# The first loads of an encoder step: x in contiguous blocks of 512 KB, with the first weights whole between them

## The chip, the cores and the metric

The kernel runs on one core of a Trainium2 chip. A core has a matrix engine (TensorE, PE in the profile, its weight loads PEld), three engines for elementwise work (VectorE or DVE, ScalarE or ACT, GpSimd or POOL), SyncE (SP), which here only issues transfers, and 16 DMA engines between the chip's memory and the core's own. The metric is the device time of one execution in microseconds; lower is better. The time before is the median of three runs.

## The reference

The reference is one inference step of a small streaming encoder of two layers, for 512 frames of a new stream and 8 x 16 frames of running streams: 640 tokens of 1024 channels in all.

```
layer 0: x = LN(a*x + 0.5*swiglu(x));  x = LN(a*x + [S5 | stick-breaking attention](x));  x = LN(a*x + 0.5*swiglu(x))
layer 1: x = LN(a*x + 0.5*swiglu(x));  x = LN(a*x + SSD(x));                              x = LN(a*x + 0.5*swiglu(x))
swiglu(x) = (silu(x @ w_gate) * (x @ w_up)) @ w_down        # w_gate, w_up: 1024 x 2816, w_down: 2816 x 1024
```

It returns the tokens and the states of the mixers. The change concerns the start of the first swiglu alone: the first products `x @ w_gate` and `x @ w_up`.

## The kernel before

**Tiles.** All matmuls are made in float32 precision out of three products of a narrower format: every operand `a` is split into `hi`, a rounded copy that ScalarE makes, and `lo = a - hi`, a subtraction on VectorE (`split`, L100). `mm3` (L146) then adds hi x hi, lo x hi and hi x lo in one accumulator bank. x lies in the core by channel: `xt["hi"]` and `xt["lo"]` hold 8 blocks of 128 channels (index `k`) by 640 tokens, and they are worked on in two token halves, tokens 0 to 255 and 256 to 639 (`HALVES`, L28). A weight unit is 128 output rows by 1024 input channels, 512 KB, and is loaded by `load_w` (L117) into one of four raw tiles (`RAWS`), then split in two halves of 512 columns each: half `j` serves channel blocks 4j to 4j + 3.

**Order.** The code is written out by hand. Each engine takes its instructions in program order, and a framework inserts the waits for data and for free buffers. Transfers are issued by SyncE in program order; one that waits for a free raw tile holds up those behind it. So where `load_x` and `load_w` stand in the program sets the order of the transfers, of the casts on ScalarE and of the subtractions on VectorE.

**The start.** `ffn` (L251) begins, for the first phase, with the lines L290 to L304. For the first token half, x comes by `load_x(0, ...)` (L1891) in four pieces of two channel blocks, 256 KB, each staged in a tile of the pool `h` (four buffers of 128 x 1280, which the hidden rows `ht` use later). The order of the transfers is: x blocks 0 and 1; the first half of the first w_gate unit; x blocks 2 to 5 in two pieces; the second half of that unit; x blocks 6 and 7; then whole units: w_up 0, w_gate 1, w_up 1. The casts follow in the order x 0-1, x 2-3, x 4-5, weights half 0, weights half 1, x 6-7, because `load_w` splits its halves only after both transfers and what lies between them. Then `load_rest` (L1899) loads the second token half of x in four pieces of 384 KB into raw tiles, and x by token into `yacc`.

In the memory of the chip, x by channel (`xT`, built by `_layout`) is an array of 128 rows; a row holds, for one position within its block, all 8 blocks of the first token half and then all 8 of the second: 20 KB. A piece of 256 KB is 128 runs of 2 KB, one out of each row.

The matmuls of the first projection (`by_k`) go channel block by channel block, with its three products each, so that they can begin when block 0 and half 0 of the weights are split; those of all others go product by product. Before them stand seven matmuls of the identity matrix with itself (L1914), whose result is used nowhere; the first real matmul is ordered behind them.

Of the kernel before, what the change touches and what calls it, by code (L numbers as in the profile page):

```python
# [25 lines left out]
KT = 8  # L26
NF = 22
HALVES = ((0, 256), (256, 384))  # L28
# [10 lines left out]
def kernel(ctx: ExitStack, tc: tile.TileContext, I, O, phases=PHASES):  # L39
    nc = tc.nc  # L40
# [31 lines left out]
    def bank_a():  # L72
        return bank(next(state["a"]))

    def bank_b():
        return bank(next(state["b"]))
# [7 lines left out]
    state = {"silu": None, "preload": None, "pst": bank_b}  # L84
# [15 lines left out]
    def split(hi, lo, src):  # L100
        nc.scalar.copy(hi, src)  # L101
        return nc.vector.tensor_tensor(lo, src, hi.bitcast(F32), op=ALU.subtract)  # L102

    def raw_tile():
        return pools["raw"].tile([128, 1024], F32, name="raw")
# [4 lines left out]
    def two_units():  # L110
        return pools["w"].tile([128, 2, 2, 512], F32R, name="w")
# [2 lines left out]

        return split(w[:, :, 0], w[:, :, 1], src.rearrange("p (j c) -> p j c", j=2))

    def load_w(src, rows=None, between=None):  # L117

        r = raw_tile()
        if between is None:  # L120
            nc.sync.dma_start(r, src)
        else:
            nc.sync.dma_start(r[:, :512], src[:, :512])
            between()
            nc.sync.dma_start(r[:, 512:], src[:, 512:])
        w = two_units()
        for j in range(2):
            half = r[:, 512 * j:512 * j + 512]
            if rows is None:
                split(w[:, j, 0], w[:, j, 1], half)  # L130
            else:
                nc.scalar.mul(w[:, j, 0], half, rows)
                nc.vector.scalar_tensor_tensor(w[:, j, 1], half, rows, w[:, j, 0].bitcast(F32),
                                               op0=ALU.mult, op1=ALU.subtract)
        return w[:, 0], w[:, 1]
# [22 lines left out]
    xt = {n: act.tile([128, KT, T], F32R, name="x" + n) for n in ("hi", "lo")}  # L158
# [92 lines left out]
    def ffn(i, ph, last, side=None):  # L251
# [4 lines left out]
        with ExitStack() as st:  # L256
# [34 lines left out]
            stage = lambda: wk.tile([128, 2 * T], F32, name="h", bufs=4)  # L291
            wg = {}
            if late:
                load_x(0, (0,), stage)
            for f in fs:
                between = (lambda: load_x(0, (2, 4), stage)) if late and f == 0 else None
                wg[f] = [load_w(I["w_gate"][i, f], None, between)]
                if between:
                    load_x(0, (6,), stage)
                wg[f].append(load_w(I["w_up"][i, f]))  # L300
            for f in fs:
                ht[f] = h_tile()
# [2 lines left out]
            for h in range(2):  # L305
                o, L = HALVES[h]
# [15 lines left out]
            for r in range(2):  # L322
                with tc.issue_after(state["xc"]) if "xc" in state else ExitStack():
                    w = load_w(I["w_gate"][i, 2 + r])
                first[r] = g_row()
                for c in range(2):
                    p = bank_a()[:, :Q] if r else sums[c]
                    mm3(p, [w_k(w, k) for k in range(KT)],
                        [(xh[:, k, Q * c:Q * c + Q], xl[:, k, Q * c:Q * c + Q]) for k in range(KT)])
                    state["silu"] = nc.scalar.activation(first[r][:, Q * c:Q * c + Q], p, AF.Silu).ins  # L330
# [1557 lines left out]
                    run_pend()  # L1888


    def load_x(h, ks=range(0, KT, 2), stage=raw_tile):  # L1891
        o, L = HALVES[h]
        for k in ks:
            r = stage()[:, :2 * L].rearrange("p (k c) -> p k c", c=L)
            state["load"] = nc.sync.dma_start(r.rearrange("p k c -> p (k c)"),
                                              I["xT"][:, KT * o + k * L:KT * o + (k + 2) * L]).ins
            split(xt["hi"][:, k:k + 2, o:o + L], xt["lo"][:, k:k + 2, o:o + L], r)

    def load_rest():  # L1899
        load_x(1)  # L1900
# [4 lines left out]
    late = [load_rest]  # L1905
# [5 lines left out]
    share("azay", "b")  # L1911

    pw = bank_b()
    for _ in range(7):  # L1914
        state["first"] = nc.tensor.matmul(pw[:, 0:128], ident, ident, start=True, stop=True).ins
    if "mix0" in phases and "ffn0" not in phases:
        with ExitStack() as st:
# [7 lines left out]
    for ph in phases:  # L1925
        last = ph == phases[-1]
        if ph.startswith("ffn"):
            ffn(int(ph[3]), ph, last, sides.get(ph))
        elif ph == "mix0":
            mixer0(ph, last)  # L1930
        else:
            mixer1(ph, last)
            if "ffn3" not in phases:
                with ExitStack() as st:
                    for _ in ssd_states(pool("ssd", 1, st, reuse_waits="tile")):
                        pass
# [4 lines left out]
def _layout(inp):  # L1941
    import numpy as np

    c = np.ascontiguousarray
    a = {k: np.asarray(v) for k, v in inp.items()}
    x = np.concatenate([a["x_prompt"].reshape(TP, D), a["x_sample"].reshape(T - TP, D)], 0)

    def cm(w):

        K, N = w.shape  # L1950
        return c(w.reshape(K // 128, 128, N // 128, 128).transpose(2, 1, 0, 3).reshape(N // 128, 128, K))

    def chan(v, n):
        return c(v.reshape(n, 128).T)

    def pairs(v):

        r = v.shape[2:]
        v = v.reshape((16, 2, 64) + r)
        return c(np.moveaxis(v, 0, 2).reshape((128, 16) + r))  # L1960

    xT = x.T.reshape(KT, 128, T).transpose(1, 0, 2)
    o = {"x": c(x), "xT": c(np.concatenate([xT[:, :, o:o + n].reshape(128, KT * n) for o, n in HALVES], 1))}
    o["ln_gb"] = c(np.stack([a["ln_g"].reshape(6, D), a["ln_b"].reshape(6, D)], 1))
    wg = a["ffn_w_gate"].reshape(4, D, NF * 128)
    wu = a["ffn_w_up"].reshape(4, D, NF * 128)
    o["w_gate"] = c(np.stack([cm(w) for w in wg]))
    o["w_up"] = c(np.stack([cm(w) for w in wu]))
    o["w_down"] = c(a["ffn_w_down"].reshape(4, NF, 128, D))

    w = cm(a["mix0_w_in"][0])
    order = [0, 1, 2, 3] + [4 + 4 * n + p for p in range(4) for n in range(2)]
    o["m0_in"] = c(w[order])
    o["m0_v"] = c(a["mix0_w_in"][0][:, 1536:].reshape(4, 2, 128, 512).transpose(0, 2, 1, 3).reshape(4, 128, 1024))
    o["m0_out"] = c(a["mix0_w_out"][0].reshape(8, 128, D))
    g = cm(a["s5_w_glu"][0])
    o["s5_wglu"] = c(g.reshape(2, 2, 128, 512).transpose(0, 2, 1, 3).reshape(2, 128, 1024))
    o["s5_bglu"] = chan(a["s5_b_glu"][0], 4)
    ldt = np.broadcast_to(a["s5_log_dt"][0][:, None], (32, 64))
    o["s5_par"] = c(np.stack([pairs(a["s5_a_re"][0]), pairs(a["s5_a_im"][0]), pairs(ldt)], 1))  # L1980
    cre = a["s5_c_re"][0].transpose(0, 2, 1)
    cim = a["s5_c_im"][0].transpose(0, 2, 1)
    o["s5_bc"] = c(np.stack([pairs(a["s5_b_re"][0]), pairs(a["s5_b_im"][0]), pairs(cre), pairs(cim)], 1))
    o["s5_d"] = c(a["s5_d"][0].reshape(1, 512))
    o["s5_h0"] = c(np.stack([pairs(a["state_s5_re"][0].transpose(1, 2, 0)), pairs(a["state_s5_im"][0].transpose(1, 2, 0))], 1))
    kc = a["cache_sb_k"][0][:, ::-1].reshape(8, 256, 4, 128)
    o["kcT"] = c(kc.transpose(2, 3, 0, 1))
    vc = a["cache_sb_v"][0][:, ::-1].reshape(8, 2, 128, 4, 128)
    o["vc"] = c(vc.transpose(3, 2, 0, 1, 4))

    w = a["ssd_w_in"][0]
    z, xbc, wdt = cm(w[:, :2048]), cm(w[:, 2048:5120]), w[:, 5120:]
    units = []
    for g in range(4):
        units += [xbc[16 + g], xbc[20 + g]] + [xbc[4 * g + q] for q in range(4)] + [z[4 * g + q] for q in range(4)]
    o["m1_in"] = c(np.stack(units))
    o["m1_dt"] = c(wdt.reshape(8, 128, 32).transpose(1, 0, 2).reshape(128, 256))
    o["m1_out"] = c(a["ssd_w_out"][0].reshape(16, 128, D))
    cwb = np.concatenate([a["ssd_conv_w"][0], a["ssd_conv_b"][0][None]], 0)
    o["conv_wb"] = c(cwb.reshape(5, 24, 128).transpose(2, 1, 0))  # L2000
    o["conv_st"] = c(a["state_conv"][0].reshape(8, 3, 24, 128).transpose(3, 2, 0, 1).reshape(128, 24, 24))
    dsk = np.repeat(a["ssd_d"][0], 64)
    o["ssd_ch"] = c(np.stack([chan(dsk, 16), chan(a["ssd_norm_g"][0], 16)], 1))
    o["ssd_hd"] = c(np.stack([a["ssd_dt_bias"][0], a["ssd_a_log"][0]], 1))
    o["ssd_h0"] = c(a["state_ssd"][0].reshape(8, 4, 512, 128).transpose(1, 0, 3, 2))
    return o
# [43 lines left out]
```

## Time and profile before

| | us |
|---|---|
| median of 3 runs (lowest, highest) | 2527.58 (2524.32, 2527.81) |
| the profiled execution, its own time | 2523.28 |
| its span, first to last instruction | 2521.6 |
| TensorE busy | 2483.8 |
| VectorE busy | 2011.8 |
| ScalarE busy | 1272.6 |
| first idle matmul of the identity starts | 1.59 |
| first matmul of the projection starts | 8.43 |
| mean granted TensorE clock | 0.998 |

The profile is one execution. Times within it count from the start of the span. In a row of the timeline stand the start, the length, the engine, the line, the operation, the written tile and the read ones with their shapes, a count, and in brackets the idle time of the engine before it with what ended it. Most lines of the first microseconds are those of helpers: L101 is the cast and L102 the subtraction of `split`, L153 the matmul of `mm3`.

### The profile page before, as it was taken

What the parts mean: (1) busy time and instruction counts of PE and PEld (TensorE: products, weight loads), DVE (VectorE), ACT (ScalarE), POOL (GpSimd) and SP (SyncE); (2) the same over time, 40 slices, a digit from 0 to 9 for tenths busy, and PEclk for the clock granted to TensorE, in tenths of its full rate; (3) what the DMA queues carried; (4) which work ended last, traced back from release to release, by engine and by line L of the source; (5) the groups of instructions that cost most, each with busy time, mean ns of one, the idle gap of its engine ahead of it and who ended that gap; (6) DMA issues with size and microseconds to landing.
All of it is one profiled execution on the core that took longest, in us unless ns stands there. A gap on an engine that the chain in (4) does not pass through costs nothing. (4 is left out here: it accounts for less than half of the span.)

```text
span 2521.6 us, 40821 instructions
## 1 busy us (share of the span) xinstructions
PE 2483.8 (99%) x15555; PEld 2281.2 (90%) x15555; DVE 2011.8 (80%) x3507; ACT 1272.6 (50%) x2390; POOL 378.7 (15%) x493
## 2 busy tenths in 40 slices
PE   9999999999999999999999999999999999999998
PEld 8999999878789999999999999999989879999997
DVE  7788777676879888877988887777586789998887
ACT  4444344336744555553455554566565544554542
POOL 0000001210130000013000001311121152211121
PEclk9999999999999999999999999999999999999999
DMA  5332334443222433452144434456464723455563
GB/s 187 109 101 79 115 116 158 145 151 118 86 77 67 115 106 98 113 157 74 59 113 113 115 105 134 150 164 199 150 215 135 244 74 100 155 148 168 154 171 115
DMA packets 178517, 324.80 MB, mean 129 GB/s; under 512 B 21344, under 2 KB 90976, under 8 KB 177808
## 3 DMA queue, kind: packets, MB, share of 16 engines
q1 hardware_dynamic: 164464, 293.83, 36.5%
q0 software_dynamic: 13856, 28.35, 5.8%
q8 instruction: 122, 2.00, 0.3%
q14 instruction: 75, 0.61, 0.1%
HBM read 259.56 MB, written 40.54 MB: 119 GB/s over the span
## 5 line engine op out<-in xcount | busy, mean ns | idle before, releaser
L101 ACT CAST w<-raw 128x512 fp32r<-128x512 f32 (+1 forms) x721 | 533.7, 771 | 332.4 <-DVE raw L376 143.4
L102 DVE TENSOR_TENSOR w<-raw,w 128x512 fp32r<-128x512 f32 (+2 forms) x721 | 621.2, 883 | 85.7 <-ACT w L101 82.8
L393 PE MATMUL bank<-xhi,w 128*128 128x320 f32 x2432 | 436.0, 309 | 2.2 <-DVE s L435 1.4
L393 PE MATMUL bank<-T,w 128*128 128x320 f32 x2736 | 428.3, 309 | 3.5 <-ACT bank L410 1.5
L393 PEld LDWEIGHTS bank<-T,w 128*128 128x128 f32 x2736 | 406.8, 188 | 6.7 <-ACT bank L410 4.2
L393 PEld LDWEIGHTS bank<-xhi,w 128*128 128x128 f32 x2432 | 376.7, 188 | 6.4 <-DVE s L435 2.2
L153 PE MATMUL bank<-xhi,w 128*128 128x256 f32 (+2 forms) x2272 | 362.8, 310 | 6.3 <-ACT w L101 3.5
L153 PEld LDWEIGHTS bank<-xhi,w 128*128 128x128 f32 x2272 | 335.9, 188 | 15.9 <-issue 4.6
L153 PE MATMUL bank<-w,h 128*128 128x512 f32 (+1 forms) x1500 | 346.5, 389 | 0.2 <-DVE yacc L239 0.2
L153 PEld LDWEIGHTS bank<-w,h 128*128 128x128 f32 x1500 | 277.8, 188 | 57.5 <-ACT h L101 1.6
L393 PE MATMUL bank<-xlo,w 128*128 128x320 f32 x1216 | 227.7, 309 | 0.0
L376 DVE TENSOR_TENSOR raw<-raw 128x512 f32<-128x512 f32 x304 | 214.2, 704 | 3.4
L393 PEld LDWEIGHTS bank<-xlo,w 128*128 128x128 f32 x1216 | 190.8, 188 | 0.0
L153 PE MATMUL bank<-xlo,w 128*128 128x256 f32 (+2 forms) x1136 | 190.4, 308 | 0.0
L542 POOL DMA_DIRECT2D yacc<-ev x84 | 72.8, 898 | 690.8 <-ACT ev L541 624.4
L153 PEld LDWEIGHTS bank<-xlo,w 128*128 128x128 f32 x1136 | 171.6, 187 | 0.6
L529 PE MATMUL bank<-w,h 128*128 128x512 f32 x576 | 134.5, 389 | 0.0
L529 PEld LDWEIGHTS bank<-w,h 128*128 128x128 f32 x576 | 107.8, 188 | 22.8 <-DVE yacc L538 0.6
L406 ACT COPY mx<-bank 128x320 f32<-128x320 f32 x152 | 64.7, 426 | 105.8 <-PE bank L393 104.9
L239 DVE SCALAR_TENSOR_TENSOR yacc<-bank,yacc 128x512 f32<-128x512 f32 x118 | 80.5, 687 | 39.7 <-PE bank L153 39.0
L538 DVE SCALAR_TENSOR_TENSOR yacc<-bank,yacc 128x512 f32<-128x512 f32 x84 | 57.9, 689 | 67.4 <-PE bank L529 67.4
L153 PE MATMUL bank<-w,og 128*128 128x512 f32 x432 | 104.6, 398 | 0.0
(442 smaller groups left out, 3360.0 us busy)
## 6 DMA issues: line engine op xcount, KB each, us to landing
raw<-in_w_up_dram SPq DMA_DIRECT2D x88, 512.0 KB, 3.9
raw<-in_w_down_dram SPq DMA_DIRECT2D x88, 512.0 KB, 3.6
raw<-in_w_gate_dram SPq DMA_DIRECT2D x87, 512.0 KB, 3.6
raw<-in_m_in_dram SPq DMA_DIRECT2D x52, 512.0 KB, 4.5
yacc<-ev POOLq DMA_DIRECT2D x84, 256.0 KB, 4.7
raw<-in_m_out_dram SPq DMA_DIRECT2D x24, 512.0 KB, 4.8
csb<-cs_d SPq DMA_DIRECT2D x20, 512.0 KB, 5.0
h<-in_ssd_h_dram SPq DMA_DIRECT2D x16, 512.0 KB, 6.4
```

The source lines that it names most:

```text
L101: nc.scalar.copy(hi, src)
L102: return nc.vector.tensor_tensor(lo, src, hi.bitcast(F32), op=ALU.subtract)
L153: state["pe"] = nc.tensor.matmul(ps, a, b, start=(k == 0), stop=(k == n - 1)).ins
L239: state["acc"] = nc.vector.scalar_tensor_tensor(ya, pb, scale, ya, op0=ALU.mult, op1=ALU.add).ins
L376: V.tensor_tensor(o, v, w, op=ALU.subtract)
L393: nc.tensor.matmul(ps, A[p][:, a, k * 128:k * 128 + 128], X[p][b][:, k, :], start=(first and n == 0), stop=(n == 11), skip_group_check=True)
L406: nc.scalar.copy(e[n], ps)
L529: nc.tensor.matmul(ps, a[:, u], b[:, v], start=(first and n == 0), stop=(n == 5), skip_group_check=True)
L538: V.scalar_tensor_tensor(ya, ps, 0.5 / ALPHA, ya, op0=ALU.mult, op1=ALU.add)
L542: nc.gpsimd.dma_start(yacc[:, t, 512 * j:512 * j + 512], e, accum_op=ALU.add)
```

## The change

x by channel is stored so that each transfer is one contiguous block: two blocks of 4 channel blocks (512 KB) for the first token half, four blocks of 2 channel blocks (384 KB) for the second. The first token half is loaded in these two transfers, each into one staging tile, and split by two casts and two subtractions of the old shape. The first w_gate unit is loaded whole, between the two. So the transfers are x 0-3, w_gate 0, x 4-7, w_up 0, w_gate 1, w_up 1; the casts go x 0-1, x 2-3, weights half 0, weights half 1, x 4-5, x 6-7. `load_w` loses the argument that let other loads stand between its two halves. Nine matmuls of the identity stand at the start instead of seven.

```diff
-    def load_w(src, rows=None, between=None):
+    def load_w(src, rows=None):
 
         r = raw_tile()
-        if between is None:
-            nc.sync.dma_start(r, src)
-        else:
-            nc.sync.dma_start(r[:, :512], src[:, :512])
-            between()
-            nc.sync.dma_start(r[:, 512:], src[:, 512:])
+        nc.sync.dma_start(r, src)
...
             if late:
-                load_x(0, (0,), stage)
+                load_x(0, (0,), 4, stage)
             for f in fs:
-                between = (lambda: load_x(0, (2, 4), stage)) if late and f == 0 else None
-                wg[f] = [load_w(I["w_gate"][i, f], None, between)]
-                if between:
-                    load_x(0, (6,), stage)
+                wg[f] = [load_w(I["w_gate"][i, f])]
+                if late and f == 0:
+                    load_x(0, (4,), 4, stage)
                 wg[f].append(load_w(I["w_up"][i, f]))
...
-    def load_x(h, ks=range(0, KT, 2), stage=raw_tile):
+    def load_x(h, ks=range(0, KT, 2), n=2, stage=raw_tile):
         o, L = HALVES[h]
         for k in ks:
-            r = stage()[:, :2 * L].rearrange("p (k c) -> p k c", c=L)
-            state["load"] = nc.sync.dma_start(r.rearrange("p k c -> p (k c)"),
-                                              I["xT"][:, KT * o + k * L:KT * o + (k + 2) * L]).ins
-            split(xt["hi"][:, k:k + 2, o:o + L], xt["lo"][:, k:k + 2, o:o + L], r)
+            r = stage()[:, :n * L]
+            src = I["xT"][128 * (KT * o + k * L):128 * (KT * o + (k + n) * L)]
+            state["load"] = nc.sync.dma_start(r, src.rearrange("(p c) -> p c", p=128)).ins
+            r = r.rearrange("p (k c) -> p k c", c=L)
+            for m in range(0, n, 2):
+                c = slice(k + m, k + m + 2)
+                split(xt["hi"][:, c, o:o + L], xt["lo"][:, c, o:o + L], r[:, m:m + 2])
...
-    for _ in range(7):
+    for _ in range(9):
         state["first"] = nc.tensor.matmul(pw[:, 0:128], ident, ident, start=True, stop=True).ins
...
-    o = {"x": c(x), "xT": c(np.concatenate([xT[:, :, o:o + n].reshape(128, KT * n) for o, n in HALVES], 1))}
+    o = {"x": c(x), "xT": c(np.concatenate([xT[:, k:k + n, o:o + L].reshape(-1)
+                                                  for (o, L), n in zip(HALVES, (4, 2)) for k in range(0, KT, n)]))}
```

## The prediction

> **What bounds the kernel now.** I read the page first, then the waits of TensorE, then the first 25 us engine by engine, and last the granted clock in single windows.
>
> ```profile
> span 2521.6 us, 40821 instructions
> ...
> PE 2483.8 (99%) x15555; PEld 2281.2 (90%) x15555; DVE 2011.8 (80%) x3507; ACT 1272.6 (50%) x2390; POOL 378.7 (15%) x493
> ```
>
> TensorE is busy for 99% of the span: 2521.6 - 2483.8 = 38 us are idle. The change only touches code that runs in the first microseconds, so it can only work on the idle time there and on the pace there. The waits of TensorE in the first 30 us, and its busy time once its stream has begun (columns of the second view: stretch, its length, PE busy, instructions, granted clock, DMA share, GB/s):
>
> ```profile
> PE bank L153 <- ACT w L101: 3.5, 1, 3.5
> PE bank L153 <- DVE w L102: 0.2, 1, 0.2
> ```
>
> ```profile
> 9.23:60.00 50.77, 50.77 (x321) 1.00 0.53 187
> 60.00:200.00 140.00, 139.87 (x854) 1.00 0.32 102
> ```
>
> From 9.23 us to 60 us TensorE never stops, and to 200 us it loses 0.13 us. So what the first projection gains passes on to what follows, as long as no later operand comes out late. The timeline of TensorE (start, length, line):
>
> ```profile
> 1.59 3.36 PE L1915 MATMUL bank<-ident 128*128 128x128 f32 x14 [1.59 <-POOL ident masks.py:199]
> 8.43 0.58 PE L153 MATMUL bank<-xhi,w 128*128 128x256 f32 x1 [3.48 <-ACT w L101]
> 9.23 0.58 PE L153 MATMUL bank<-xhi,w 128*128 128x256 f32 x1 [0.22 <-DVE w L102]
> ...
> 11.75 0.63 PE L153 MATMUL bank<-xhi,w 128*128 128x256 f32 x2
> ...
> 12.81 0.28 PE L153 MATMUL bank<-xlo,w 128*128 128x256 f32 x1
> ...
> 13.61 1.98 PE L153 MATMUL bank<-xhi,w 128*128 128x256 f32 x16
> ...
> 21.77 0.51 PE L153 MATMUL bank<-xhi,w 128*128 128x384 f32 x2
> ```
>
> Seven idle matmuls (14 instructions, 0.24 us each) end at 4.95; the first real one starts at 8.43 and the continuous stream at 9.23. One more thing is to be read here: two matmuls of 256 columns take 0.63 us at 11.75, with steps of 0.21 us from one to the next ((12.81 - 11.75)/5), and sixteen later take 1.98, 0.12 each. TensorE runs at half pace until about 12.8. What holds the first matmul is seen on ScalarE and VectorE:
>
> ```profile
> 3.98 0.62 ACT L101 CAST xhi<-h 128x512 fp32r<-128x512 f32 x1 [1.89 <-DMA h<-in_xT_dram]
> 5.96 0.62 ACT L101 CAST xhi<-h 128x512 fp32r<-128x512 f32 x1 [1.36 <-DMA h<-in_xT_dram]
> 7.24 0.62 ACT L101 CAST xhi<-h 128x512 fp32r<-128x512 f32 x1 [0.66 <-DMA h<-in_xT_dram]
> 7.76 1.34 ACT L101 CAST w<-raw 128x512 fp32r<-128x512 f32 x2
> 9.11 0.62 ACT L101 CAST xhi<-h 128x512 fp32r<-128x512 f32 x1
> 10.40 3.67 ACT L101 CAST w<-raw 128x512 fp32r<-128x512 f32 x6 [0.67 <-DMA raw<-in_w_up_dram]
> ...
> 18.18 1.56 ACT L101 CAST xhi<-raw 128x768 fp32r<-128x768 f32 x2
> ```
>
> ```profile
> 8.49 1.33 DVE L102 TENSOR_TENSOR w<-raw,w 128x512 fp32r<-128x512 f32 x2
> 9.76 0.69 DVE L102 TENSOR_TENSOR xlo<-h,xhi 128x512 fp32r<-128x512 f32 x1
> ```
>
> The weights' cast stands behind three casts of x in ScalarE's order, and the third x piece arrives only at 7.24. From the start of the weights' cast it is 8.43 - 7.76 = 0.67 us to the first matmul and 9.23 - 7.76 = 1.47 us to the stream (the subtraction on VectorE in between).
>
> **The change, part by part.** The loads first: SyncE's issues, and the time from issue to landing of single transfers (last column, us).
>
> ```profile
> 0.81 0.39 SPq L1895 DMA_DIRECT2D h<-in_xT_dram  x1
> 1.25 0.42 SPq L123 DMA_DIRECT2D raw<-in_w_gate_dram  x1
> ...
> 3.61 0.43 SPq L121 DMA_DIRECT2D raw<-in_w_up_dram  x1
> ```
>
> ```profile
> h<-in_xT_dram SPq DMA_DIRECT2D x1, 256.0 KB, 3.2
> ...
> raw<-in_w_gate_dram SPq DMA_DIRECT2D x1, 256.0 KB, 3.3
> ...
> raw<-in_w_up_dram SPq DMA_DIRECT2D x1, 512.0 KB, 6.8
> ```
>
> So 256 KB had landed at 0.81 + 3.2 = 4.0, 512 KB at 1.25 + 3.3 = 4.55, 1024 KB at 7.24 (the third x cast's wait), 1536 KB by 9.1, 2048 KB at 3.61 + 6.8 = 10.4. What the DMA engines moved between:
>
> ```profile
> 3.50:5.00 1.50, 1.45 (x7) 1.00 0.86 212
> ...
> 8.00:11.00 3.00, 2.35 (x9) 1.00 1.02 414
> ```
>
> At nearly equal busy share the early stretch moves half as much. There pieces of x lie in the queue, each 2 KB per partition out of a row of 20 KB; later whole weight units of 4 KB per partition.
>
> Issues: six transfers ahead of the first w_up unit become three, about 0.45 us of SyncE each, so w_up's issue moves from 3.61 to about 0.81 + 3 x 0.46 = 2.2; what stands behind on that queue is issued 1.4 us earlier. Worth nothing by itself, since the DMA engines have work throughout.
>
> First x block, 512 KB instead of 256 KB: it lands as late as the first 512 KB did, 4.55. The two casts of x can then start 0.57 us later than the first did, at 4.55 and, casts of this shape following each other by 7.76 - 7.24 = 0.52, at 5.07; ScalarE is free at 5.6. This costs nothing while the weights land after 5.6.
>
> First weights whole, second in the queue, so at 1024 KB in all. Upper end: 7.24 as before. Lower end: 512 KB at the late rate, 524/414 = 1.27 us after 4.55, that is 5.82. How a compact block of x fares the trace does not show; compact weights reach 414 GB/s, but not at the start of the program. I take the middle, 6.4 (an estimate). The stream then starts at 6.4 + 1.47 = 7.87 instead of 9.23: **1.36 us earlier**, between 0.52 (7.24, only the third x cast taken out from ahead of the weights) and 1.94.
>
> One rule speaks on this term: the Trainium skill, page "DMA: Bandwidth & Descriptors" (Specifications), puts the ceiling of all 16 engines at 435 GB/s; the late row is close to it, the early one at half. At that ceiling for the whole of the first megabyte the weights would land before ScalarE is free, and the stream would start at about 5.6 + 1.47 = 7.07 (an estimate).
>
> x channels 4 to 7 after the weights: 1536 KB, at worst 9.1 as before; cast to 9.7 and subtracted to 10.5. At half pace channels 0 to 3 take TensorE from 7.87 to 7.87 + 11 x 0.21 = 10.2. So at worst the stream waits 0.3 us, and by the middle (about 8, 6.4 plus the mean of 1.27 and the 9.1 - 7.24 = 1.9 of before) not at all: 0. The next unit, w_up, is cast from 10.4 at the latest and its subtraction is needed after the 24 + 8 matmuls of gate: no wait.
>
> Second token half: four blocks of 384 KB, same bytes per partition, same slots. They wait for a raw tile, which VectorE frees after the weights' subtraction, and come about as much earlier as that. The casts of x end at 19.7, the matmuls that read them begin at 21.77: 2 us of cover, and both move together. 0.
>
> Two staging tiles of the pool instead of four: the two tiles of the first hidden rows take fresh buffers instead of reused ones; nothing waits there today. 0.
>
> Two more idle matmuls: 4 x 0.24 = 0.96 us, ending at 5.91, ahead of the first real one at 7.07 (5.82 + 0.67 = 6.49 at the lower end). They delay nothing; what they do to the pace is the last term. The granted clock, in windows of 3.41 us (PE busy in the third column, clock in the fifth; in the first windows the column holds 1.00, but the pace above says half):
>
> ```profile
> 2.55:5.96 3.41, 2.40 (x12) 1.00 0.91 281
> ```
>
> ```profile
> 664.73:668.14 3.41, 0.64 (x12) 1.00 0.49 165
> 668.14:671.55 3.41, 3.41 (x14) 0.50 0.00 0
> ...
> 2026.65:2030.06 3.41, 1.66 (x21) 1.00 0.11 31
> 2030.06:2033.47 3.41, 3.41 (x9) 0.50 0.45 123
> ```
>
> ```profile
> 1753.41:1756.83 3.42, 2.01 (x12) 1.00 0.83 283
> 2081.06:2084.48 3.42, 2.03 (x18) 1.00 0.04 7
> 575.93:579.34 3.41, 2.07 (x16) 1.00 0.00 0
> 2156.15:2159.56 3.41, 2.15 (x15) 1.00 0.23 28
> ```
>
> Windows with 0.64 and 1.66 us of work were followed by exactly one window at half clock; those with 2.01 or more were not. Counting back from 668.14 in steps of 3.413, 192 of them end at 12.8, where the pace doubles: so the same grid rules the start, and the window 2.55 to 5.96 with 2.40 busy did not open the clock. On this grid the changed kernel has the idle matmuls in that window from 2.55 to 5.91, 3.36 of 3.41, which I take as enough: full pace from 5.96. The next window, to 9.37, holds 0.11 + 9.37 - 7.87 = 1.61 us of work, just under the 1.66 that closed it: half pace from 9.37 to 12.78. Work done by 12.78, in full-pace time: 1.50 + 3.41/2 = 3.21, against (12.78 - 9.23)/2 = 1.78 before. **Gain 1.43 us**. If the idle matmuls do not open the clock: (12.78 - 7.87)/2 = 2.46, gain 0.68. The grid will lie otherwise in another execution; I take 1.4 as the sum.
>
> **The sum.** The profiled execution took 2523.28 us, its span 2521.6; less 1.4 gives 2521.9. The runs shown have a median of 2527.58, 4.3 above that execution, and all four together a mean of 2525.75. Less 1.4 these give 2526.2 and 2524.35; I take the point between, **2525.2**.
>
> **The rivals.**
>
> *The clock stays open.* If TensorE's work of 1.61 us between 5.96 and 9.37 is enough, or the weights land by 6.0 (then it is over 2.0, which the rows show to be enough), full pace holds from the first real matmul: 12.78 - 7.87 - 1.78 = 3.1 us gained, with weights at 6.0 3.5. Time: 2525.75 - 3.3 = 2522.5 to 2527.58 - 3.3 = 2524.3. For it: the margin is 0.05 us. Against: the weights' landing must be in the faster half. The Trainium skill, page "TensorE: Matmul & The Clock Gate" (Part 1), has the clock fall back only after a whole idle window; by that the gate would stay open here and the gain would be 3.1. The row of 2026.65 disagrees: 1.66 us of work, and half clock after it.
>
> *Nothing lands earlier.* If the early 212 GB/s come from the start of the program and not from the pieces, the weights land at 7.24, the stream starts at 8.71, and on a grid that does not favour it the gain is (9.23 - 8.71)/2 = 0.3: 2527.3. For it: the first x piece, alone in the queue, took 3.2 us too. Against: six transfers become three.
>
> *Slower, by the clock later on.* The four windows of 2.01 to 2.15 us busy are near the closing point. If the shift of all work against the grid puts each a few tenths lower (the point lies between 1.66 and 2.01), each costs 3.41/2 = 1.7 us: four cost 6.8, less 1.4 is 5.4 slower, 2533.0. For it: two windows closed already. Against: the idle gaps there are as long as before, and a shifted grid can as well free the two that close now, 3.4 us.
>
> **How the numbers follow.** The forecast has 0.60, the open clock 0.20, nothing earlier 0.14, slower 0.06. What this kernel's measurement can tell from no change is 0.2%, 5 us. Below 2522.5 lie a tenth of the forecast's cases (the runs shown differ by 3.5 us among themselves) and a quarter of the open clock's: faster 0.11. Above 2532.6 half of the slow case and a little else: slower 0.04. The same 0.85. Range: from the open clock on a low run, 2520.5, to nothing gained on a high one, 2529.
>
> **What would show it.** The timeline of ScalarE: casts x, x, weights, weights, x, x, the third starting at about 6.4 (5.8 to 7.3). TensorE: 18 idle instructions to 5.9, the stream from 7.9 (7.3 to 8.7) without a wait of over 0.3 us; the pace in the first channels, 0.64 or 0.34 us per channel, tells the clock. The start of the second token half's matmuls, at 21.77 before, shows the whole gain of this stretch: 20.4 by the forecast, 18.5 with the clock open. Wrong I am if TensorE waits anew between 9 and 200 us, if x's second block comes after 9.1, or if that start moves and the end does not.

## The result, and the profile after

The changed kernel takes 2523.0 us in the median of 22 runs, the kernel before 2526.53 in 22 runs beside them: a ratio of 0.9987, 95% interval 0.9982 to 0.9993, some 3.3 us faster (1.8 to 4.5). The ratio leaves out one run of the kernel before that took 6671 us. A second set of runs (below) gave 0.9992, 0.9983 to 1.0002. So the first set shows a gain of about a thousandth, inside the 0.2% that was called "the same"; the second set alone would not set it apart from nothing.

The profiled execution of the changed kernel took 2521.54 us, 1.74 less than that of the kernel before. Its page begins:

```profile
span 2519.8 us, 40822 instructions
...
PE 2480.4 (98%) x15559; PEld 2278.3 (90%) x15559; DVE 2013.5 (80%) x3507; ACT 1269.7 (50%) x2390; POOL 376.8 (15%) x493
```

TensorE's timeline (L1912 is the idle matmul now, L148 the matmul of `mm3`, line numbers being a few lower than before):

```profile
1.59 4.21 PE L1912 MATMUL bank<-ident 128*128 128x128 f32 x18 [1.59 <-POOL ident masks.py:199]
6.64 0.38 PE L148 MATMUL bank<-xhi,w 128*128 128x256 f32 x1 [0.84 <-ACT w L101]
7.37 0.38 PE L148 MATMUL bank<-xhi,w 128*128 128x256 f32 x1 [0.34 <-DVE w L102]
...
8.74 0.39 PE L148 MATMUL bank<-xhi,w 128*128 128x256 f32 x2
...
18.27 1.20 PE L148 MATMUL bank<-xhi,w 128*128 128x384 f32 x6
19.76 2.01 PE L148 MATMUL bank<-xhi,w 128*128 128x384 f32 x10 [0.29 <-ACT xhi L101]
...
40.17 2.62 PE L148 MATMUL bank<-xhi,w 128*128 128x320 f32 x16 [0.91 <-DVE hf L309]
```

The stream begins at 7.37 instead of 9.23, and from its first matmul on at full pace: two matmuls take 0.39 us, where they took 0.63. The second token half begins at 18.27 instead of 21.77, 3.5 us earlier. Then come two waits that the kernel before did not have, 0.29 us for x and 0.91 us for `hf`, and the group that began at 41.93 begins at 40.17, 1.76 us earlier: half of the 3.5 us is gone.

ScalarE's casts, in the new order:

```profile
4.54 1.14 ACT L101 CAST xhi<-h 128x512 fp32r<-128x512 f32 x2 [2.45 <-DMA h<-in_xT_dram]
5.97 1.14 ACT L101 CAST w<-raw 128x512 fp32r<-128x512 f32 x2 [0.29 <-DMA raw<-in_w_gate_dram]
7.25 1.14 ACT L101 CAST xhi<-h 128x512 fp32r<-128x512 f32 x2
8.53 3.69 ACT L101 CAST w<-raw 128x512 fp32r<-128x512 f32 x6
```

Time from issue to landing of the three transfers (issued at 0.82, 1.27 and 1.74), and what the DMA engines moved, in the same stretches as before (the last column is GB/s):

```profile
h<-in_xT_dram SPq DMA_DIRECT2D x1, 512.0 KB, 3.7
...
raw<-in_w_gate_dram SPq DMA_DIRECT2D x1, 512.0 KB, 4.7
...
h<-in_xT_dram SPq DMA_DIRECT2D x1, 512.0 KB, 5.5
```

```profile
3.50:5.00 1.50, 1.50 (x9) 1.00 1.02 401
5.00:6.50 1.50, 0.80 (x4) 1.00 1.02 391
```

Where 212 GB/s were moved, 401 are now. The granted clock, in the windows of this execution's grid (PE busy in the third column):

```profile
2.48:5.89 3.41, 3.32 (x16) 1.00 0.97 359
5.89:9.30 3.41, 2.31 (x17) 1.00 1.03 416
```

The idle matmuls fill the first window and open the clock at 5.89; the second, with 2.31 us of work, keeps it open.

The new wait at 40 us hangs on VectorE. Its rows after:

```profile
27.20 3.91 DVE L102 TENSOR_TENSOR w<-raw,w 128x512 fp32r<-128x512 f32 x6 [3.89 <-ACT w L101]
...
39.57 0.55 DVE L309 TENSOR_TENSOR hf<-bank,hf 128x384 f32<-128x384 f32 x1
```

and those of before, with TensorE's group behind them:

```profile
28.93 0.69 DVE L102 TENSOR_TENSOR w<-raw,w 128x512 fp32r<-128x512 f32 x1 [4.32 <-ACT w L101]
...
40.98 0.56 DVE L315 TENSOR_TENSOR hf<-bank,hf 128x384 f32<-128x384 f32 x1
...
41.93 2.51 PE L153 MATMUL bank<-xhi,w 128*128 128x320 f32 x16
```

TensorE cannot reuse a bank before VectorE has multiplied `hf` out of it. Before, that product ended at 41.54 and the matmul began at 41.93: no wait, and 0.39 us of margin. VectorE has hardly any free time between its first split of w_gate 2 and that product, so the product moves with the arrival of w_gate 2. The split begins only 1.73 us earlier (27.20, before 28.93); five loads of x by token, 2.6 MB, stand ahead of w_gate 2 in the queue. The product ends only 1.42 us earlier (40.12, before 41.54), because one more operation of VectorE now stands ahead of it (shown below by the kernel before with nine idle matmuls).

### The profile page after: what moved, and what is told of

It is laid out like the page before. It is cut to its first block, busy times and chain, and to the rows that moved or that the text cites. A ratio compares the mean times of both kernels' runs of the same rounds, so it can differ in the third digit from the quotient of the medians.

```text
span 2519.8 us, 40822 instructions
## 1 busy us (share of the span) xinstructions
PE 2480.4 (98%) x15559; PEld 2278.3 (90%) x15559; DVE 2013.5 (80%) x3507; ACT 1269.7 (50%) x2390; POOL 376.8 (15%) x493
## 5 line engine op out<-in xcount | busy, mean ns | idle before, releaser
L148 PE MATMUL bank<-xhi,w 128*128 128x256 f32 (+2 forms) x2272 | 361.3, 310 | 5.0 <-DVE yacc L1832 1.4
L148 PEld LDWEIGHTS bank<-xhi,w 128*128 128x128 f32 x2272 | 334.3, 187 | 15.0 <-issue 3.7
L148 PE MATMUL bank<-w,h 128*128 128x512 f32 (+1 forms) x1500 | 346.5, 389 | 0.2 <-DVE yacc L234 0.2
L148 PEld LDWEIGHTS bank<-w,h 128*128 128x128 f32 x1500 | 277.8, 188 | 57.6 <-ACT h L101 1.6
L148 PE MATMUL bank<-xlo,w 128*128 128x256 f32 (+2 forms) x1136 | 189.8, 308 | 0.0
L148 PEld LDWEIGHTS bank<-xlo,w 128*128 128x128 f32 x1136 | 170.9, 187 | 0.6
L148 PE MATMUL bank<-w,og 128*128 128x512 f32 x432 | 103.0, 393 | 0.0
```

What stands on the lines that cost most here:

```text
L148: state["pe"] = nc.tensor.matmul(ps, a, b, start=(k == 0), stop=(k == n - 1)).ins
```

## The experiments

What all thirteen profiles show of the first 42 us, out of TensorE's timelines (start of the first real matmul, of the stream, of the second token half, of the group of 320 columns that began at 41.93):

| kernel | first | stream | second half | group | ratio to before (95%) |
|---|---|---|---|---|---|
| before | 8.43 | 9.23 | 21.77 | 41.93 | |
| changed | 6.64 | 7.37 | 18.27 | 40.17 | 0.9987 (0.9982 to 0.9993) |
| changed, seven idle | 6.46 | 7.19 | 19.73 | 41.65 | 0.9997 (0.9988 to 1.0005) |
| changed, x in rows | 6.60 | 7.33 | 19.85 | 41.69 | 0.9995 (0.9986 to 1.0003) |
| before, nine idle | 8.28 | 9.08 | 21.61 | 41.93 | 1.0002 (0.9994 to 1.0011) |
| before, x in blocks | 8.11 | 8.92 | 22.77 | 43.06 | 1.0004 (0.9995 to 1.0012) |
| changed, x by token later | 6.41 | 7.13 | 18.38 | 40.67 | 0.9990 (0.9982 to 0.9999) |
| changed, eleven idle | 6.42 | 7.15 | 18.83 | 40.14 | 0.9987 (0.9979 to 0.9996) |
| both of these | 6.43 | 7.16 | 18.92 | 40.61 | 0.9994 (0.9985 to 1.0002) |
| before, x by token later | 8.44 | 9.25 | 22.71 | 42.87 | 1.0000 (0.9991 to 1.0008) |
| changed, x by token last | 6.38 | 7.11 | 19.34 | 39.49 | 0.9986 (0.9978 to 0.9995) |
| that with eleven idle | 6.39 | 7.12 | 18.78 | 39.27 | 0.9987 (0.9978 to 0.9995) |
| changed, again | 6.44 | 7.16 | 18.05 | 39.60 | 0.9992 (0.9983 to 1.0002) |

Each row is one execution, so the columns of times show mechanisms; the ratio is of 11 or 12 runs (22 for the changed kernel). Where TensorE does not wait in between, the group follows the second half's start by 20.16 us (kernel before) to 20.49 us (the last copy with eleven idle matmuls).

**Theory and rivals.** The first theory: the gain at the start has three sources, loads that land sooner because x is compact, one cast less ahead of the weights, and a clock that opens in the idle matmuls and stays open over a short wait; and VectorE's chain behind w_gate 2 then takes half of it back. The rivals: the idle matmuls alone, or the loads alone; and for the loss at 40 us, the slightly different order of VectorE's subtractions.

### Parts of the change alone

Seven idle matmuls in the changed kernel:

```diff
-    for _ in range(9):
+    for _ in range(7):
         state["first"] = nc.tensor.matmul(pw[:, 0:128], ident, ident, start=True, stop=True).ins
```

> The changed kernel with seven idle matmuls instead of nine; all else as changed. If the idle matmuls keep the clock open over the wait for the weights (the first theory), they end at 4.95, the wait before the first real matmul is about 1.7 us, the first channels run at 0.64 us each on most grids, the second token half starts near 20 us instead of 18.3, and the time is 0.5 to 1.5 us above the changed kernel's (ratio to before about 0.9992). If the earlier loads alone make the gain (the rival), the ratio stays at 0.9987 and the stream still starts at 7.4.

The clock in the windows of its grid:

```profile
1.07:4.48 3.41, 2.88 (x13) 1.00 0.73 235
4.48:7.89 3.41, 1.39 (x10) 1.00 0.98 370
7.89:11.31 3.42, 3.42 (x19) 0.50 1.02 411
```

The stream starts as early as in the changed kernel (7.19), so that part belongs to the loads. On this grid seven idle matmuls do open the clock, but the wait behind them is 1.7 us long, the next window holds only 1.39 us of work, and one window at half clock follows. The second half starts at 19.7, as the first theory had it, and the ratio is 0.9997 (about 0.9992 was expected). But the window at half clock is not what holds the group at 41.65: without a wait it would have come at 19.73 + 20.16 = 39.9.

```profile
28.34 0.62 ACT L101 CAST w<-raw 128x512 fp32r<-128x512 f32 x1 [5.82 <-DMA raw<-in_w_gate_dram]
```

```profile
41.65 2.61 PE L148 MATMUL bank<-xhi,w 128*128 128x320 f32 x16 [1.61 <-DVE hf L309]
```

The loads are those of the changed kernel, yet w_gate 2 is cast at 28.34 instead of 26.54, and TensorE waits 1.61 us for `hf`. Why the same loads land so far apart stays open. The intervals of 0.9997 and 0.9987 overlap, so it is not shown that nine idle matmuls are better than seven, neither by the times nor by the start of the group.

The changed kernel with x in rows of 20 KB, as before:

```diff
-            src = I["xT"][128 * (KT * o + k * L):128 * (KT * o + (k + n) * L)]
-            state["load"] = nc.sync.dma_start(r, src.rearrange("(p c) -> p c", p=128)).ins
+            state["load"] = nc.sync.dma_start(r, I["xT"][:, KT * o + k * L:KT * o + (k + n) * L]).ins
...
```

(The array in memory is laid out as in the kernel before.)

> The changed kernel with x stored in rows of 20 KB as before, so that the same three transfers of 512 KB read runs of 4 KB out of the rows; order and idle matmuls as changed. If compact storage makes the early loads fast (first theory), the weights land about 0.5 to 1.2 us later than 5.97 and the stream starts at 7.9 to 8.6 instead of 7.37. If longer runs and fewer transfers are what counts (rival), it starts within 0.2 us of 7.37.

Its casts, then its clock:

```profile
4.66 1.14 ACT L101 CAST xhi<-h 128x512 fp32r<-128x512 f32 x2 [2.57 <-DMA h<-in_xT_dram]
5.93 1.14 ACT L101 CAST w<-raw 128x512 fp32r<-128x512 f32 x2
7.21 1.14 ACT L101 CAST xhi<-h 128x512 fp32r<-128x512 f32 x2
```

```profile
1.18:4.59 3.41, 3.00 (x14) 1.00 0.77 243
4.59:8.01 3.42, 1.76 (x12) 1.00 1.02 416
8.01:11.42 3.41, 3.41 (x18) 0.50 0.95 375
```

Here the first theory fell: 4.66, 5.93 and 7.21 are the changed kernel's 4.54, 5.97 and 7.25. The compact storage, which the title names first, does nothing that these profiles show. The later second half of this copy (19.85) comes from the clock: opened in the middle of the idle matmuls, it made the rest of them short, they ended at 5.29, the wait grew to 1.31 us, and 1.76 us of work did not keep the clock open. Its group, at 41.69, hangs on w_gate 2 again, cast at 28.05, with a wait of 1.52 us for `hf`.

The kernel before, with nine idle matmuls:

```diff
-    for _ in range(7):
+    for _ in range(9):
```

> The kernel before with nine idle matmuls instead of seven, nothing else. The idle matmuls end at 5.9 and the first real one stays at 8.4, a wait of 2.5 us. If the clock needs a short wait as well (first theory), it closes again on most grids and the ratio is within 0.9995 to 1.0002. If the idle matmuls are the whole change (rival), the ratio is near 0.999 and the first channels run at 0.34 us each.

```profile
2.84:6.26 3.42, 2.96 (x14) 1.00 0.94 296
6.26:9.67 3.41, 0.97 (x6) 1.00 1.00 364
9.67:13.08 3.41, 3.41 (x19) 0.50 0.90 328
```

The clock opens, the wait of 2.5 us follows, and it closes: nothing gained (1.0002). The rival of the idle matmuls alone is out.

This run also shows what the order of VectorE's operations is worth:

```profile
28.95 3.92 DVE L102 TENSOR_TENSOR w<-raw,w 128x512 fp32r<-128x512 f32 x6 [4.71 <-ACT w L101]
...
39.72 0.48 DVE L359 TENSOR_TENSOR h<-xhi,h 128x320 f32<-128x320 f32 x1
...
41.33 0.55 DVE L315 TENSOR_TENSOR hf<-bank,hf 128x384 f32<-128x384 f32 x1
```

The split of w_gate 2 begins as in the kernel before (28.95, there 28.93), but `h<-xhi,h` now stands ahead of the `hf` product, which ends at 41.88 instead of 41.54. All nine profiles with nine or eleven idle matmuls have this order, the four with seven do not. So the rival of the order holds in part: it is worth 0.34 us, about a third of the 0.91 us that the changed kernel waits at 40 us.

The kernel before, with x in contiguous blocks of its own 256 KB:

```diff
-            state["load"] = nc.sync.dma_start(r.rearrange("p k c -> p (k c)"),
-                                              I["xT"][:, KT * o + k * L:KT * o + (k + 2) * L]).ins
+            src = I["xT"][128 * (KT * o + k * L):128 * (KT * o + (k + 2) * L)]
+            state["load"] = nc.sync.dma_start(r.rearrange("p k c -> p (k c)"), src.rearrange("(p c) -> p c", p=128)).ins
...
```

(The array in memory is laid out in these blocks.)

> The kernel before with x stored in contiguous blocks of its own transfers of 256 KB; order, halved weights and seven idle matmuls as before. If compact storage makes the early loads fast (first theory), the third cast of x begins 0.7 us or more before 7.24 and the stream starts at 8.0 to 8.6 instead of 9.23. If the size of the runs counts (rival: 2 KB before, 4 KB after), the stream stays within 0.2 us of 9.23. By both, the time is 0 to 1 us under before's.

The stream starts at 8.92, 0.16 earlier than in the kernel before with nine idle matmuls, whose loads are the old ones, and 0.31 earlier than in the kernel before. That is neither what the theory had (8.0 to 8.6) nor the rival (within 0.2 us of 9.23). The executions with old loads differ among themselves by 0.17 us (9.08 to 9.25), and between 3.5 and 5.0 us this copy moved 240 GB/s, within the 206 to 259 of theirs; the ratio is 1.0004. So a few tenths of a microsecond may come from compact storage at runs of 2 KB, which one execution cannot tell; the 1.9 us of the changed kernel do not. What is left for the earlier stream is what both the changed kernel and its copy with rows have: three transfers of 4 KB per partition instead of six of 2 KB, and the order of loads and casts. These were not taken apart.

### Where the gain goes at 40 us

The loads of x by token behind w_gate 2 and 3:

```diff
-        nc.sync.dma_start(r, src)
+        state["load"] = nc.sync.dma_start(r, src).ins
...
                     w = load_w(I["w_gate"][i, 2 + r])
+                if r == 1 and ph == PHASES[0]:
+                    load_yacc()
                 first[r] = g_row()
...
     def load_rest():
         load_x(1)
+        if phases[0] != "ffn0":
+            load_yacc()
+
+    def load_yacc():
         with tc.issue_after(state["load"]):
...
```

(`load_yacc` takes over the loads of x by token from `load_rest`, and orders them behind the last load before it.)

> The changed kernel with the five loads of x by token (2.6 MB into yacc) issued after the loads of w_gate 2 and 3 instead of ahead of them. If those loads hold up w_gate 2 and with it VectorE's chain, and that chain takes back the gain at 41 us (first theory), then VectorE begins the split of w_gate 2 before 22 us instead of 27.2, TensorE no longer waits for hf at 40 us, the third matmul group of 320 columns starts at 39.0 to 40.0 instead of 40.2, and the ratio to before is 0.9980 to 0.9986. If the gain is lost to the other order of VectorE's subtractions (rival), TensorE still waits 0.9 us or more there and the ratio stays at 0.9987. A third case: the later x by token comes after 55 us and TensorE waits for its accumulators.

VectorE, ScalarE and TensorE:

```profile
20.80 2.64 DVE L102 TENSOR_TENSOR w<-raw,w 128x512 fp32r<-128x512 f32 x4
...
30.31 1.29 DVE L102 TENSOR_TENSOR w<-raw,w 128x512 fp32r<-128x512 f32 x2 [4.59 <-ACT w L101]
...
40.06 0.55 DVE L309 TENSOR_TENSOR hf<-bank,hf 128x384 f32<-128x384 f32 x1
```

```profile
29.66 1.14 ACT L101 CAST w<-raw 128x512 fp32r<-128x512 f32 x2 [5.06 <-DMA raw<-in_w_down_dram]
```

```profile
40.67 2.61 PE L148 MATMUL bank<-xhi,w 128*128 128x320 f32 x16 [1.64 <-DVE hf L309]
```

Half a hit. w_gate 2 and 3 are split at 20.8, as expected, but TensorE waits longer than in the changed kernel, 1.64 us, and the group and the ratio (0.9990) miss what the theory had. The third case, a wait for the accumulators, did not come. VectorE's next work in its order is the split of w_down 0, and that now comes behind the 2.6 MB: it idles 4.59 us for it. The wait had been put on the wrong weights; it is the whole bundle of w_gate 2, 3 and w_down 0, 1 that must be there.

Eleven idle matmuls in the changed kernel (`range(11)`), and both edits together:

> The changed kernel with eleven idle matmuls instead of nine. They end at 6.3 to 6.9, up to the first real matmul at 6.6. If an unbroken stretch of work opens the clock on every grid (first theory), the first channels take 0.34 us each, the second token half starts at 18.2 to 18.6, and the time equals the changed kernel's within 0.5 us, since VectorE's chain is the bound at 41 us. If the start alone sets the time (rival), it is 0.5 to 1.5 us under the changed kernel's.

> Both: x by token after w_gate 2 and 3, and eleven idle matmuls. If VectorE's chain was the bound at 41 us and is no longer (first theory), the start's gain now passes on: the group at 41.9 us before starts at 38.5 to 39.5, and the ratio is 0.9978 to 0.9985, the best of all. If not (rival), it is that of the changed kernel, 0.9987.

With eleven the wait before the first matmul is 0.35 us and the clock open throughout; the second half starts at 18.83, later than the 18.2 to 18.6 expected, with a wait of 0.16 us for x at 9.06 on the way. The group starts at 40.14, as with nine, after a wait of 0.67 us for `hf`, and the ratio is the same: at 40 us VectorE's chain decides, not the start. Both together miss the 0.9978 to 0.9985 that was expected (0.9994, group at 40.61), for the reason just seen.

The kernel before, with x by token behind w_gate 2 and 3:

> The kernel before with the loads of x by token after w_gate 2 and 3, nothing else changed. TensorE did not wait there before, so by the first theory nothing is gained: the stream starts at 9.1 to 9.3, the group at 41.9 stays within 0.3 us, ratio 0.9996 to 1.0003. If the later loads help by themselves (rival), for example by x of the second token half or w_gate arriving earlier, the ratio is 0.9993 or less.

The ratio is 1.0000, as expected: where TensorE does not wait, earlier weights are worth nothing. Its group at 42.87 misses the 0.3 us expected around 41.93, because its clock was at half until 14.8:

```profile
11.36:14.77 3.41, 3.41 (x18) 0.50 0.79 228
```

x by token behind w_down 0 and 1 as well:

```diff
...
                     wd[f] = load_w(I["w_down"][i, f])
+                if fs[0] == 0 and ph == PHASES[0]:
+                    load_yacc()
...
```

> The changed kernel with the loads of x by token after w_down 0 and 1 too, so that nothing but weights comes ahead of them. If what held VectorE's chain in the last runs was w_down 0 and 1, which came behind the 2.6 MB of x by token (first theory), VectorE has no idle time of over 2 us waiting for weights between 20 and 33 us, TensorE does not wait for hf at 40 us, and the group at 41.93 us before starts at 38.7 to 39.3, 2.6 to 3.2 us earlier; the time is 0.8 to 1.5 us under the changed kernel's of the same runs. If VectorE's own work between 30 and 40 us is the bound whatever lands (rival), TensorE still waits 0.6 us or more there and the group starts at 40 to 40.7.

```profile
25.48 1.29 DVE L102 TENSOR_TENSOR w<-raw,w 128x512 fp32r<-128x512 f32 x2
...
38.26 0.55 DVE L309 TENSOR_TENSOR hf<-bank,hf 128x384 f32<-128x384 f32 x1
```

```profile
7.70 0.63 PE L148 MATMUL bank<-xhi,w 128*128 128x256 f32 x2
...
39.49 2.51 PE L148 MATMUL bank<-xhi,w 128*128 128x320 f32 x16
```

w_down 0 is split at 25.5 instead of 30.3, `hf` is done at 38.8, and TensorE does not wait, although in this execution the first channels ran at half pace (0.63 us for two). From the second half's start to the group it takes 39.49 - 19.34 = 20.15 us, like the kernel before (41.93 - 21.77 = 20.16), where the changed kernel took 21.9. So the wait at 40 us is mainly the arrival of weights behind x by token: with it removed, and VectorE's operations still in the changed kernel's order at that place, there is no wait. One reservation: the second half began 1.07 us later here than in the changed kernel. From a start at 18.27 TensorE would need the bank at 18.27 + 20.16 = 38.43 (an estimate), 0.4 us ahead of this `hf`; no run shows the whole 3.5 us passing on. The group missed the 38.7 to 39.3 expected, and in time this copy could not be told from the changed kernel: 2522.21 against 2522.84 in the same runs, 0.6 less where 0.8 to 1.5 was expected.

> The same with eleven idle matmuls. By the first theory the group starts at 38.7 to 39.5 on every grid of the clock, so the median is at or up to 0.5 us under that of the run with nine. By the rival it is that of the changed kernel.

> The changed kernel itself, for comparison within the same runs. Ratio to before 0.9982 to 0.9993 as measured. Its profile shows how much of it hangs on the grid of the clock: with the clock closed for one window after the first matmuls, the second token half starts near 19.8 instead of 18.3, and the group at 41 us still near 40.2 to 41.7, since VectorE's chain sets it.

With eleven idle matmuls too, the group starts at 39.27, the earliest of all, and the median is 2521.56, lowest of all; the interval (0.9978 to 0.9995) does not set it apart from the changed kernel either. The changed kernel again gave 2522.84, ratio 0.9992, with the clock open from 5.1 on in its profile. That execution shows why single times differ by more than what is sought here. A wait of 2.3 us for a transfer in the middle of the program, then the clock in the windows around it:

```profile
PE bank L1713 <- DMA bx<-bcx_d: 2.3, 1, 2.3
```

```profile
1752.72:1756.14 3.42, 1.33 (x8) 1.00 1.00 320
1756.14:1759.55 3.41, 3.17 (x15) 0.50 0.85 268
1759.55:1762.96 3.41, 3.41 (x18) 0.50 0.22 66
1762.96:1766.38 3.42, 3.42 (x18) 0.50 0.88 272
```

Three windows at half clock cost about 5 us there, and the span is 2525.6.

## Why the prediction was right or wrong

**The time and the sign.** 2525.2 was forecast, 2520.5 to 2529; measured were 2523.0 against 2526.53. "The same, within 0.2%" held. The forecast gain of 1.4 us lies below the 1.8 to 4.5 measured. The two profiled executions differ by 1.74 us, close to 1.4, but that is luck: two errors nearly cancel. The start gained 3.5 us instead of 1.4, because the clock stayed open, and half of that did not pass on. The time itself is the one that the first rival gave, 2522.5 to 2524.3 with a chance of 0.20, but that rival too let the whole gain pass on.

Why the medians differ by more than the profiled pair is not shown. Half of the changed kernel's runs, 11 of 22, had a granted clock of 0.999, against 12 of the 97 runs of the kernel before beside the experiments; at equal clock (0.997, 0.998, 0.999) the two differ by 2.2, 0.6 and 2.4 us on average.

**First x block.** 4.55 forecast, cast at 4.54. It cost nothing, as said.

**First weights.** 6.4 was taken as the middle of 5.82 and 7.24, which is 6.53; the cast began at 5.97. The term was mis-sized by 0.4 us: it was the lower end, 512 KB at the late rate, that came. In the nine executions with these three transfers the cast begins at 5.71 to 5.97, and only in this one did ScalarE wait for the weights (0.29 us); in the others it came straight behind ScalarE's own casts of x. The rival that nothing lands earlier is out: 401 GB/s in the stretch that had 212. The reason given, pieces out of rows of 20 KB, was wrong in one half: rows do not matter, the copy with rows landed alike.

By the Trainium skill's page "DMA: Bandwidth & Descriptors" (Specifications), 435 GB/s is the ceiling; the early stretch, now at 401, lies below it, which agrees.

**The stream's start.** 7.87 forecast, 7.37 measured: 0.43 of the difference is the weights, the rest VectorE, which was free at once (0.73 us from matmul to matmul instead of 0.80).

**The clock.** The sum had it close again at 9.37 with 1.61 us of work in the window; the execution had 2.31, and it stayed open. This was the first rival, and its number for the start of the second half was 18.5, against 18.27. On other grids the sum's own case happened: the copies with seven idle matmuls and with rows closed for one window at 1.39 and 1.76 us. With nine idle matmuls and x by token last, too, the clock opened only at 10.0. So the mechanism was right, and which case falls depends on where the grid lies in an execution.

The Trainium skill's page "TensorE: Matmul & The Clock Gate" (Part 1) says that the clock falls back after an idle window. Three more rows here disagree: windows with 0.97, 1.39 and 1.76 us of work were followed by half clock.

**What passes on.** This step failed: "From 9.23 us to 60 us TensorE never stops ... so what the first projection gains passes on to what follows, as long as no later operand comes out late." One did. The second half's start moved by 3.5 us, the group's by 1.76. The rows said that TensorE never waited, which is not the same as having margin: it was 0.39 us at 41.9. With `hf` itself 1.42 us earlier, about 1.8 us can pass there (an estimate). The forecast's own 1.4 would have passed; the rival's 3.1 to 3.5 could not. The loads did come earlier by about as much as the weights did, as was said of the second token half: its first block was issued at 7.95 instead of 9.85, and w_gate 2's split began 1.73 us earlier. But TensorE moved by the 1.86 us of its stream and by another 1.64 from its clock, and the loads have no part in that. The sign of being wrong that was named, a new wait of TensorE between 9 and 200 us, came.

**x channels 4 to 7, the idle matmuls, the staging tiles.** No wait, as said; 5.80 for the end of the idle matmuls, 5.91 forecast. x's second token half was given "2 us of cover, and both move together": the cover went (a wait of 0.29 us), since TensorE moved by 3.5 and the last of the four blocks came late, 5.8 us after its issue.

**Slower, by the clock later on.** The mechanism exists, as the windows at 1756 us show, and runs with a lower granted clock are longer: of the changed kernel's 22, the eleven at 0.999 took 2521.0 us on average, the six at 0.997 took 2524.7. But the change did not make it more frequent: 0.997 or less in 6 of these 22 runs, and in 49 of the 97 of the kernel before beside the experiments.

## What to carry to other kernels

A stretch in which the bounding engine never waits does not say how far its start can be moved: take the last operand of each stage. The time between its end and its use, and the time by which the operand itself will come earlier, are what a shift may have (0.39 and 1.42 us here, of 3.5). When the start is sped up, the loads that the next stage waits for have to move ahead of those that are needed later: with x by token last, the wait at 40 us was gone, though the time did not show it. Idle matmuls that warm the clock have to reach close to the first real one: behind waits of 1.31, 1.68 and 2.47 us the clock closed again, behind 0.84 and 0.91 us it stayed open.

## What the runs showed of the hardware that had not been expected

The clock's two points can be bounded from these windows of 3.41 us. A closed clock stayed closed after 2.40 and 2.82 us of work in a window and opened after 2.96 and 3.00; 2.88 opened it in one execution and not in another. An open one closed after 1.76 and stayed open after 2.01 and more. The 2.82 is from the run with x by token last, the 2.88 that did not open it from the one of before with x in blocks:

```profile
3.17:6.58 3.41, 2.82 (x14) 1.00 0.98 390
```

```profile
7.80:11.22 3.42, 2.88 (x12) 1.00 1.02 413
```

Busy times of single matmuls are modelled, so these bounds are good to some tenths of a microsecond.

How x lies in memory, in runs of 4 KB side by side or 20 KB apart, made no difference to when it landed (4.54, 5.97, 7.25 against 4.66, 5.93, 7.21), while six transfers with 2 KB per partition moved little more than half as much per time as three with 4 KB at the start of the program: 206 to 259 GB/s between 3.5 and 5.0 us in four executions, 388 to 423 in nine. Whether the length of the runs or the number of transfers does it stays open.
